# A two-layer decoder trunk on one core: transposes of queries, keys and attention weights move from TensorE to VectorE and the DMA queues

## The chip, the core and the metric

The kernel runs on one core of a Trainium2 chip, in one launch. The metric is the device time of the launch in microseconds, lower is better. All arithmetic is float32 at the interface; the large products are made of float32r parts.

## What is computed

One sequence of 256 tokens, width 2048. Layer 0 is a gated token mixer with a feed-forward part (width 5632, causal convolution of width 3); layer 1 is an attention with forget gates and a feed-forward part of the same kind. The change concerns the attention of layer 1, cut here to what it computes:

```python
kvf = rmsnorm(h, kv_norm) @ w_kvf            # keys, values and 16 forget gates, one side for all
k, v, f = ...                                # 16 heads of 128
k = rmsnorm(k, k_norm)                       # per head
c = cumsum(log_sigmoid(f + b_f))             # one row of 256 sums per head
q, g = split(rmsnorm(h, b_norm) @ w_qg)
q = rmsnorm(q, q_norm)                       # per head
for i in range(2):                           # query blocks of 128 tokens
    s = q[i] @ k[:hi].T * 128**-0.5 + c[t] - c[s]
    p = softmax(where(s_index <= t_index, s, -inf))
    o[i] = p @ v[:hi]
h = h + (o * sigmoid(g)) @ w_out
```

## The kernel before

**The stream.** All weights pass through one list of chunks, each 128 x 1024 floats (512 KB), in the order in which they are used. `Stream.run` goes through the list once. In its turn i it issues the load of chunk i+6 (line 70, on SyncE's queue, into one of four buffers `raw`), splits chunk i+3 (lines 82 and 83: ScalarE writes the high part `whi`, VectorE the low part `wlo` = raw - whi, four buffers each), emits the products of chunk i on TensorE (line 166), and then takes every pending generator one step further (`advance`). A generator's step is all it emits up to its next `yield`. So the place of every other instruction, on each engine and on the queues, is set by the turn in which its generator reaches it, and each engine works through its own list in that order. The load of chunk i+6 needs the buffer of chunk i+2, so it waits until VectorE has split that one.

**The products.** Each is high x high, low x high and high x low. In a token block (512 output columns for all 256 tokens, 8 chunks, 12 matmuls of 512 columns per chunk) the second matmul of a chunk already reads the low part.

**The attention.** The stages, in order: four token blocks of queries (`b_q`), one small chunk of forget gates (`kvf_f`), four blocks of keys (`kvf_k`), four of values (`kvf_v`), then the output gates (`b_g`, 8 groups of 4 chunks) and the output projection (`b_out`). Beside the first query chunks `kv_operand` prepares the second operand `att_X` from the residual `h`, one of 16 rows of blocks per turn (`prep`, lines 258 and 259). `forget_sums` makes the gates' sums on VectorE in many small steps (lines 609 to 644), during the first 20 turns of the keys.

**Norm of queries and keys.** When a block of queries or keys is done, `head_norm` squares its first 128 tokens on ScalarE (line 561), reduces and takes the reciprocal root on VectorE (lines 564 to 567, small operations), and scales out of PSUM (line 569). Two turns later TensorE transposes the four heads by matmuls with the identity `ident` (line 575) into a small PSUM bank `mp`, and ScalarE copies them, times the norm's gain, to `att_q` or `att_k` (line 576). In the turn after that the same begins for the second 128 tokens.

**Heads.** `heads` starts one generator `one_head` every second turn, as soon as the head's values are there. A head: fetch its row of sums broadcast to all partitions (line 650, GpSimd's queue), the bias of sums and mask in `L` (lines 655 to 658), scores on TensorE (660, 661), softmax (663 to 671), three transposes of the weights on TensorE (676) and their copy to `att_pT` on ScalarE (678), output on TensorE (683 to 685), its copy over the head's queries in `att_q` (686). Each head takes three of the two rotating `mp` banks in turn. The output gates (`g_done`) wait until all 16 heads are done, then follow one per turn.

## Time and profile before

| what | value |
|---|---|
| median of 3 runs | 2210.79 us (2210.58 to 2210.93) |
| the profiled execution, its own time | 2210.51 us |
| its span in the trace | 2208.8 us |
| granted TensorE clock | 0.999 |
| busy: PE, DVE, ACT, POOL | 2199.4, 1465.0, 1154.1, 19.0 us |
| query and key blocks, 1003 to 1192 us | PE 189.0, DVE 143.4, ACT 93.2 us busy |
| values and heads, 1192 to 1342 us | PE 150.0, DVE 91.9, ACT 91.2 us busy |

How to read it: PE is TensorE's matmuls, PEld its weight loads, DVE VectorE, ACT ScalarE, POOL GpSimd, SP SyncE; a q behind a name (SPq) is that engine's instruction queue, where DMAs are issued. In a row of a group stand the line of the kernel, the engine, the operation, output and inputs, shapes and the count; behind the bar the busy time in us and the mean of one in ns; behind the second bar the idle time just before, with what ended it. In a timeline a row begins with start and length in us. Matmuls overlap in the pipeline, so a step from one start to the next says more than a length. In a row of a stage (`A:B`) stand its length and then busy time and count for PE, PEld, DVE, ACT and POOL, the clock, the DMA engines' busy share and GB/s. DMA rows end with the median time from issue to landing.

### The profile page before, as it was taken

The page shows a single profiled execution, that of the slowest core. Times are in us where ns is not written, and L with a number is a line of the kernel's source. Part 1 is how long each engine was busy: PE and PEld are TensorE (multiplying, and loading weights), DVE is VectorE, ACT ScalarE, POOL GpSimd, SP SyncE. Part 2 cuts the span into 40 slices and gives each one's busy share as a digit, 9 for nine tenths or more (in the row PEclk, how much of TensorE's full clock was granted, in tenths as well). Part 3 has the DMA queues.
Part 4 walks back from the last instruction along what each step waited for, and adds up shares of the span by engine and source line. Part 5 has one row for each costly group of instructions (what it writes and reads, how often), then busy time and mean ns, then how long its engine had stood idle before and what let it go on. Part 6 is the DMA issues. An engine that isn't in the chain of part 4 may idle for free.

```text
span 2208.8 us, 41643 instructions
## 1 busy us (share of the span) xinstructions
PE 2199.4 (100%) x17208; PEld 2105.5 (95%) x17208; DVE 1465.0 (66%) x2107; ACT 1154.1 (52%) x1549; POOL 19.0 (1%) x41
## 2 busy tenths in 40 slices
PE   9999999999999999999999999999999999999998
PEld 7899999999999999998788888999999999999998
DVE  6676677777777755557786566667777777765553
ACT  5545455555555544345444666556555555544443
POOL 0000000000000000000000110000000000000000
PEclk9999999999999999999999999999999999999999
DMA  8555565556555655665565555656556565655653
GB/s 304 178 192 178 195 196 196 192 194 197 192 191 195 197 191 184 207 192 172 174 186 185 173 163 184 195 189 195 191 194 196 187 198 194 198 192 194 195 192 134
DMA packets 116910, 422.70 MB, mean 191 GB/s; under 512 B 13280, under 2 KB 13680, under 8 KB 116464
## 3 DMA queue, kind: packets, MB, share of 16 engines
q1 hardware_dynamic: 115776, 417.93, 57.8%
q8 instruction: 134, 2.20, 0.4%
q0 software_dynamic: 768, 2.10, 0.4%
q14 instruction: 56, 0.46, 0.1%
q10 hardware_dynamic: 176, 0.02, 0.0%
HBM read 417.88 MB, written 2.11 MB: 190 GB/s over the span
## 4 chain that ended last, share of the span: by engine, by line
PE 99%; DMA 0%; DVE 0%; ACT 0%; ACTq 0%; issue 0%; SPq 0%; DVEq 0%
PE ps L166 96%; PE mp L166 1%; DMA raw<-a_in_v 0%; PE mp L489 0%; PE mp L575 0%; PE mp L661 0%; PE mp L676 0%; PE mp L685 0%; PE mp L684 0%; PE mp L660 0%; PE mp L683 0%; PE mp L350 0%; DVE h L402 0%; DVE wlo L83 0%; ACT whi L82 0%; ACTq L811 0%
## 5 line engine op out<-in xcount | busy, mean ns | idle before, releaser
L83 DVE TENSOR_TENSOR wlo<-raw,whi 128x1024 fp32r<-128x1024 f32 (+1 forms) x787 | 954.8, 1219 | 461.1 <-ACT whi L82 459.3
L82 ACT ACTIVATE whi<-raw 128x1024 fp32r<-128x1024 f32 (+1 forms) x787 | 826.8, 1056 | 670.9 <-PE ps L166 602.4
L166 PE MATMUL ps<-X,whi 128*128 128x256 f32 (+1 forms) x6176 | 827.8, 286 | 0.0
L166 PEld LDWEIGHTS ps<-X,whi 128*128 128x128 f32 x6176 | 758.3, 188 | 16.5
L166 PE MATMUL ps<-X,wlo 128*128 128x256 f32 x3328 | 445.5, 276 | 0.0
L166 PEld LDWEIGHTS ps<-X,wlo 128*128 128x128 f32 x3328 | 413.2, 188 | 5.5
L166 PE MATMUL ps<-ffn_H,whi 128*128 128x256 f32 (+1 forms) x2696 | 342.9, 277 | 0.0
L166 PEld LDWEIGHTS ps<-ffn_H,whi 128*128 128x128 f32 x2696 | 322.7, 188 | 1.1
L166 PE MATMUL ps<-ffn_H,wlo 128*128 128x256 f32 x1364 | 186.6, 276 | 0.0
L166 PEld LDWEIGHTS ps<-ffn_H,wlo 128*128 128x128 f32 x1364 | 170.2, 188 | 0.4
L166 PE MATMUL ps<-whi,att_X 128*128 128x512 f32 x512 | 168.1, 400 | 0.0
L523 DVE SCALAR_TENSOR_TENSOR ffn_c<-ffn_a,col,ffn_c 128x255 f32<-128x255 f32 x352 | 162.0, 481 | 6.3
L166 PE MATMUL ps<-whi,X 128*128 128x512 f32 x512 | 161.6, 395 | 0.5 <-ACT whi L82 0.5
L519 ACT ACTIVATE ffn_c<-ffn_a,col 128x256 f32<-128x256 f32 x176 | 96.4, 595 | 49.8 <-DVE ffn_a L316 49.8
L166 PEld LDWEIGHTS ps<-whi,X 128*128 128x128 f32 x512 | 96.0, 188 | 21.9 <-ACT whi L82 1.2
L166 PEld LDWEIGHTS ps<-whi,att_X 128*128 128x128 f32 x512 | 96.2, 188 | 20.4
L316 DVE TENSOR_TENSOR ffn_a<-ps,rB 128x512 f32<-128x512 f32 x74 | 51.2, 692 | 96.7 <-PE ps L166 96.7
L166 PE MATMUL ps<-wlo,X 128*128 128x512 f32 x256 | 99.4, 391 | 0.8 <-DVE wlo L83 0.8
L166 PE MATMUL ps<-wlo,att_X 128*128 128x512 f32 x256 | 100.0, 390 | 0.0
L258 ACT ACTIVATE X<-h,col 128x256 fp32r<-128x256 f32 x64 | 29.1, 501 | 84.4 <-DVE h L322 67.8
L166 PE MATMUL ps<-att_X,whi 128*128 128x256 f32 (+2 forms) x520 | 68.9, 281 | 0.0
L166 PEld LDWEIGHTS ps<-att_X,whi 128*128 128x128 f32 (+1 forms) x520 | 61.5, 185 | 2.2
(160 smaller groups left out, 1156.3 us busy)
## 6 DMA issues: line engine op xcount, KB each, us to landing
raw<-up SPq DMA_DIRECT2D x352, 512.0 KB, 3.4
raw<-down SPq DMA_DIRECT2D x176, 512.0 KB, 4.1
raw<-a_in_u SPq DMA_DIRECT2D x32, 512.0 KB, 3.9
raw<-a_out SPq DMA_DIRECT2D x32, 512.0 KB, 4.2
raw<-b_q SPq DMA_DIRECT2D x32, 512.0 KB, 4.2
raw<-kvf_k SPq DMA_DIRECT2D x32, 512.0 KB, 4.2
raw<-kvf_v SPq DMA_DIRECT2D x32, 512.0 KB, 4.0
raw<-b_g SPq DMA_DIRECT2D x32, 512.0 KB, 3.3
```

Of the source, the lines that this page charges most:

```text
L82: self.nc.scalar.activation(hi[:, :n], raw, AF.Copy)
L83: self.nc.vector.tensor_tensor(lo[:, :n], raw, hi[:, :n].bitcast(F32), op=OP.subtract)
L166: nc.tensor.matmul(o, a, b, start=start, stop=stop, skip_group_check=True)
L258: nc.scalar.activation(dst[:, kt, :T], h[:, kt, :], AF.Copy, scale=g)
L316: nc.vector.tensor_tensor(a, src, rB[:, None, :].to_broadcast([P, 2, T]), op=OP.mult)
L519: nc.scalar.activation(c[:, m, :], a[:, m, :], AF.Identity, scale=w[2], bias=column(C_CONVB + l * 2 * KF + f))
L523: nc.vector.scalar_tensor_tensor(c[:, m, n:], a[:, m, :T - n], w[k], c[:, m, n:], op0=OP.mult, op1=OP.add)
```

## The change

Three things are done. First, the transposes leave TensorE. `blocks_turned` transposes on VectorE in blocks of 32 x 32, which turns each block but leaves the blocks where they are; `exchange` moves the blocks between groups of 32 partitions by way of a DRAM buffer `way`: four writes of 32 partitions each, in the next turn, and one read in the turn after, all on SyncE's queue. Keys land directly in `att_k` (in an order of 32-token blocks, which the score matmuls read with strides); queries land in a buffer `att_rows` of 128 x 512, and ScalarE copies them to `att_q` three turns after the read, times the product of both norms' gains (`att_gain`, made once); weights land in `att_rows` and are read by the output matmuls directly.

Second, `head_norm` has one `yield` where there were three: the transpose of the first 128 tokens and the norm of the second 128 follow in the turn after the first norm.

Third, `one_head` and `heads` become one generator. It takes two turns per head, starts when the keys are done (before, a head waited for its values), fetches the row of sums for the next head ahead, and emits in the first turn of head n the output of an earlier head (at most n-3) ahead of the scores of n, two outputs per round once all scores are out. The output gates of heads 2p and 2p+1 wait for those two heads only. GpSimd's descriptor scratch is set to 4096 bytes.

```diff
-    def head_norm(key, blk, gain):
+    def blocks_turned(src, n):
+        turned = ph.temp("turned", [P, 512])[:, :n * P].rearrange("p (c h j) -> p c h j", c=4, h=n)
+        nc.vector.transpose(turned.rearrange("p c h j -> p h c j"),
+                            src.rearrange("p (h c i) -> p h c i", h=n, c=4))
+        return turned.rearrange("p c h j -> p c (h j)")
+
+    def exchange(key, turned, n, new, then):
+        way = dram.tile([4, 32, 4, n * 32], F32, name=f"way_{key}", tag=f"way_{key}")
+        for r in range(4):
+            nc.sync.dma_start(way[:, :, r, :].rearrange("c i x -> i c x"), turned[32 * r:32 * r + 32])
+        yield
+        dst = new()
+        nc.sync.dma_start(dst, way.rearrange("c i r x -> (c i) r x"))
+        yield
+        then(dst)
+
+    def head_norm(key, blk):
...
                 yield
-                yield
-                mp = misc_ps()
-                for j in range(4):
-                    nc.tensor.transpose(mp[:, j * P:(j + 1) * P], n[:, j * P:(j + 1) * P], ident)
-                nc.scalar.activation(dst[:, 4 * blk:4 * blk + 4, tb * P:(tb + 1) * P],
-                                     mp.rearrange("p (a b) -> p a b", a=4), AF.Copy, scale=column(gain))
-                yield
+                turned = blocks_turned(n, 4)
+                if key == "k":
+                    new = lambda tb=tb: att("k").rearrange("p b t h j -> p b t (h j)")[:, blk, 4 * tb:4 * tb + 4]
+                    s.start(exchange(f"k{blk}{tb}", turned, 4, new, lambda dst: None))
+                else:
+                    s.start(exchange(f"q{blk}{tb}", turned, 4, lambda: four_rows(4),
+                                     lambda dst, tb=tb: s.start(q_scaled(blk, tb, dst))))
...
+    def four_rows(n):
+        return ph.temp("rows", [P, 512], bufs=6)[:, :n * P].rearrange("p (r x) -> p r x", r=4)
+
+    def q_scaled(blk, tb, rows):
+        yield
+        nc.scalar.activation(att("q")[:, 4 * blk:4 * blk + 4, tb * P:(tb + 1) * P].rearrange(
+            "p h (r j) -> p r h j", r=4), rows.rearrange("p r (h j) -> p r h j", h=4), AF.Copy, scale=att("gain"))
...
-    def one_head(hd):
...
-        mp = misc_ps()
-        for j in range(3):
-            nc.tensor.transpose(mp[:, j * P:(j + 1) * P], L[:, j, :], ident)
-        pT = ph.temp("pT", [P, 3, P])
-        nc.scalar.activation(pT, mp[:, :3 * P].rearrange("p (a b) -> p a b", a=3), AF.Copy)
...
+        while state["done"] < NH:
...
+            go = [hd for hd, _ in waiting if hd < min(state["v"], n - 2)][:2 if n >= NH else 1]
+            o = misc_ps() if go else None
+            for i, hd in enumerate(go):
+                pT = waiting.pop(0)[1]
+                oo, vv = o[:, i * T:(i + 1) * T], v[:, :, hd * P:(hd + 1) * P]
+                nc.tensor.matmul(oo[:, :P], vv[:, 0, :], pT[:, :, 0, :], start=True, stop=True)
+                nc.tensor.matmul(oo[:, P:], vv[:, 0, :], pT[:, :, 1, :], start=True, stop=False)
+                nc.tensor.matmul(oo[:, P:], vv[:, 1, :], pT[:, :, 2, :], start=False, stop=True)
+            if n < NH:
+                S = misc_ps()[:, :3 * P]
+                kk = k[:, n // 4, :, n % 4, :]
+                nc.tensor.matmul(S[:, :P], q[:, n, :P], kk[:, :4], start=True, stop=True)
+                nc.tensor.matmul(S[:, P:], q[:, n, P:], kk, start=True, stop=True)
+            for i, hd in enumerate(go):
+                nc.scalar.activation(q[:, hd, :], o[:, i * T:(i + 1) * T], AF.Copy)
+                state["done"] += 1
+            yield
...
+                s.start(exchange(f"p{n}", blocks_turned(L, 3), 3, lambda: four_rows(3),
+                                 lambda dst, n=n: waiting.append((n, dst.rearrange("p r (b j) -> p r b j", b=3)))))
...
-            while state["done"] < NH or state["gates"] < p:
+            while state["done"] < 2 * p + 2 or state["gates"] < p:
...
-    nc = bacc.Bacc("TRN2", target_bir_lowering=False, num_devices=1)
+    nc = bacc.Bacc("TRN2", target_bir_lowering=False, num_devices=1, dynamic_dma_scratch_size=4096)
```

VectorE's list at the end of the first query block, before: from the end of the first norm (line 569) to the begin of the second (line 564). `att_big` is the scaled result, `wlo` a chunk's low part, `att_X` the operand being prepared.

```order
L569 TENSOR_TENSOR att_big<-ps,att_hr 128x512
L83 TENSOR_TENSOR wlo<-raw,whi 128x1024
L259 SCALAR_TENSOR_TENSOR att_X_11579<-h,col,att_X_11579 128x256
L83 TENSOR_TENSOR wlo<-raw,whi 128x1024
L259 SCALAR_TENSOR_TENSOR att_X_11579<-h,col,att_X_11579 128x256
L83 TENSOR_TENSOR wlo<-raw,whi 128x1024
L259 SCALAR_TENSOR_TENSOR att_X_11579<-h,col,att_X_11579 128x256
L564 TENSOR_REDUCE att_hv<-sq 128x4
```

The same place after the change, from the operand's prep (line 259) to the end of the second norm and on to its transpose; the lines of the norm are now 584 to 589, the transpose is 551.

```order
L259 SCALAR_TENSOR_TENSOR att_X_11505<-h,col,att_X_11505 128x256
L551 STREAM_TRANSPOSE att_turned<-att_big 128x4x4x32
L584 TENSOR_REDUCE att_hv<-sq 128x4
...
L587 TENSOR_SCALAR att_hr<-att_hr,rcol 128x4
L589 TENSOR_TENSOR att_big<-ps,att_hr 128x512
L83 TENSOR_TENSOR wlo<-raw,whi 128x1024
L259 SCALAR_TENSOR_TENSOR att_X_11505<-h,col,att_X_11505 128x256
L551 STREAM_TRANSPOSE att_turned<-att_big 128x4x4x32
```

Between the two norms stood three low parts; now one stands there (ahead of the first row shown), and the transpose.

SyncE's list after the change, in the stage of the values: `raw` is a weight load, `way_p` a head's four writes, the row that reads `way_p` its read. Before, this stage held nothing but the 32 loads.

```order
L70 DMA raw<-kvf_v 128x1024
L559 DMA way_p_13423<-att_turned 32x4x96 x4
L70 DMA raw<-kvf_v 128x1024
L562 DMA att_rows<-way_p_13423 128x384
L70 DMA raw<-kvf_v 128x1024
L559 DMA way_p_13489<-att_turned 32x4x96 x4
```

Each head puts five DMAs between two loads and the next two: the writes behind one load, the read behind the other.

TensorE's list in a head, before: the transposes (line 676) cut through a chunk, and the output (683 to 685) and the scores of the next head (660, 661) follow behind it.

```order
L166 MATMUL ps<-whi,att_X_11579 128x512
L676 MATMUL mp<-ident,att_big 128x128 x3
L166 MATMUL ps<-whi,att_X_11579 128x512
...
L683 MATMUL mp<-att_pT,att_v 128x128
L684 MATMUL mp<-att_pT,att_v 128x128
L685 MATMUL mp<-att_pT,att_v 128x128
L660 MATMUL mp<-att_k,att_q 128x128
L661 MATMUL mp<-att_k,att_q 128x256
```

The same place after the change.

```order
L166 MATMUL ps<-whi,att_X_11505 128x512
L705 MATMUL mp<-att_rows,att_v 128x128
L706 MATMUL mp<-att_rows,att_v 128x128
L707 MATMUL mp<-att_rows,att_v 128x128
L711 MATMUL mp<-att_k,att_q 128x128
L712 MATMUL mp<-att_k,att_q 128x256
L166 MATMUL ps<-whi,att_X_11505 128x512
```

The transposes are gone from the list; output and scores stand as before, with the weights read from `att_rows`.

More of the change, by code (lines that the diff above doesn't have):

```diff
@@ L542, in att @@
         ph.open("att")
-        shape = {"X2": [P, KD, 2 * T], "q": [P, NH, T], "k": [P, NH, T], "v": [P, 2, D],
-                 "ccol": [P, 2, NH]}[key]
+        shape = {"X2": [P, KD, 2 * T], "q": [P, NH, T], "k": [P, 4, 8, 4, 32], "v": [P, 2, D],
+                 "ccol": [P, 2, NH], "gain": [P, 1]}[key]
         return ph.keep(key, shape, F32R if key == "X2" else F32)
+    def blocks_turned(src, n):
[12 more added lines that the diff above has]
+        then(dst)
     def kv_operand():
+        att("X2")
+        nc.vector.tensor_tensor(att("gain"), column(C_QNORM), column(C_KNORM), op=OP.mult)
         for _ in range(3):
@@ L552, in kv_operand @@
             yield
-    def head_norm(key, blk, gain):
+    def head_norm(key, blk):
         def done(ps):
-            dst = att(key)
             for tb in range(2):
@@ L587, in done @@
             yield
-            for hd in range(4 * blk, 4 * blk + 4):
-                state["heads"].append(hd)
+            state["v"] += 4
         return done
@@ L645, in forget_sums, with heads @@
         yield
-    def one_head(hd):
+    def heads():
         q, k, v, ccol = att("q"), att("k"), att("v"), att("ccol")
-        cB = ph.temp("cB", [P, T])
-        nc.gpsimd.dma_start(cB, cd[hd:hd + 1, :].to_broadcast([P, T]))
-        yield
-        L = ph.temp("big", [P, 512], bufs=6)[:, :3 * P].rearrange("p (a b) -> p a b", a=3)
-        mp = misc_ps()
-        S = mp[:, :3 * P]
-        nc.scalar.activation(L[:, 0, :], cB[:, :P], AF.Identity, scale=-1.0, bias=ccol[:, 0, hd:hd + 1])
-        nc.scalar.activation(L[:, 1:, :], cB.rearrange("p (a b) -> p a b", a=2), AF.Identity, scale=-1.0,
-                             bias=ccol[:, 1, hd:hd + 1])
-        nc.gpsimd.affine_select(L[:, 0::2, :], L[:, 0::2, :], pattern=[[0, 2], [-1, P]], compare_op=OP.is_ge,
-                                fill=NEG, base=0, channel_multiplier=1)
-        nc.tensor.matmul(S[:, :P], q[:, hd, :P], k[:, hd, :P], start=True, stop=True)
-        nc.tensor.matmul(S[:, P:], q[:, hd, P:], k[:, hd, :], start=True, stop=True)
-        yield
-        nc.vector.scalar_tensor_tensor(L, S.rearrange("p (a b) -> p a b", a=3), SCALE, L, op0=OP.mult, op1=OP.add)
-        mx = ph.temp("mx", [P, 2])
-        sm = ph.temp("sm", [P, 2])
-        for tb, part in ((0, L[:, 0:1, :]), (1, L[:, 1:3, :])):
-            nc.vector.tensor_reduce(mx[:, tb:tb + 1], part, axis=AX.XY, op=OP.max, negate=True)
-            nc.scalar.activation(part, part, AF.Exp, bias=mx[:, tb:tb + 1], accum_out=sm[:, tb:tb + 1])
-        nc.vector.reciprocal(sm, sm)
-        for tb, part in ((0, L[:, 0:1, :]), (1, L[:, 1:3, :])):
-            nc.vector.tensor_scalar(part, part, sm[:, tb:tb + 1], None, op0=OP.mult)
-        yield
-        yield
-        mp = misc_ps()
-        for j in range(3):
-            nc.tensor.transpose(mp[:, j * P:(j + 1) * P], L[:, j, :], ident)
-        pT = ph.temp("pT", [P, 3, P])
-        nc.scalar.activation(pT, mp[:, :3 * P].rearrange("p (a b) -> p a b", a=3), AF.Copy)
-        yield
-        mp = misc_ps()
-        o = mp[:, :T]
-        vv = v[:, :, hd * P:(hd + 1) * P]
-        nc.tensor.matmul(o[:, :P], vv[:, 0, :], pT[:, 0, :], start=True, stop=True)
-        nc.tensor.matmul(o[:, P:], vv[:, 0, :], pT[:, 1, :], start=True, stop=False)
-        nc.tensor.matmul(o[:, P:], vv[:, 1, :], pT[:, 2, :], start=False, stop=True)
-        nc.scalar.activation(q[:, hd, :], o, AF.Copy)
-        state["done"] += 1
@@ L689, in heads, with fetch @@
-    def heads():
-        n = 0
-        while n < NH:
-            if state["heads"]:
-                s.start(one_head(state["heads"].pop(0)))
-                n += 1
-                yield
-            yield
+        parts = [(0, 0, 1), (1, 1, 3)]
+        rows, waiting = {}, []
+        def fetch(hd):
+            rows[hd] = ph.temp("cB", [P, T])
+            nc.gpsimd.dma_start(rows[hd], cd[hd:hd + 1, :].to_broadcast([P, T]))
+        fetch(0)
+        yield
+        n = 0
+        while state["done"] < NH:
+            if n < NH:
+                cB = rows.pop(n)
+                L = ph.temp("big", [P, 512], bufs=6)[:, :3 * P]
+                l = L.rearrange("p (a b) -> p a b", a=3)
+                nc.scalar.activation(l[:, 0, :], cB[:, :P], AF.Identity, scale=-1.0, bias=ccol[:, 0, n:n + 1])
+                nc.scalar.activation(l[:, 1:, :], cB.rearrange("p (a b) -> p a b", a=2), AF.Identity, scale=-1.0,
+                                     bias=ccol[:, 1, n:n + 1])
+                nc.gpsimd.affine_select(l[:, 0::2, :], l[:, 0::2, :], pattern=[[0, 2], [-1, P]],
+                                        compare_op=OP.is_ge, fill=NEG, base=0, channel_multiplier=1)
+                if n + 1 < NH:
+                    fetch(n + 1)
+            go = [hd for hd, _ in waiting if hd < min(state["v"], n - 2)][:2 if n >= NH else 1]
[6 more added lines that the diff above has]
+                nc.tensor.matmul(oo[:, P:], vv[:, 1, :], pT[:, :, 2, :], start=False, stop=True)
+            if n < NH:
+                S = misc_ps()[:, :3 * P]
[5 more added lines that the diff above has]
+                state["done"] += 1
+            yield
+            if n < NH:
+                nc.vector.scalar_tensor_tensor(L, S, SCALE, L, op0=OP.mult, op1=OP.add)
+                mx = ph.temp("mx", [P, 2])
+                sm = ph.temp("sm", [P, 2])
+                for tb, a, b in parts:
+                    nc.vector.tensor_reduce(mx[:, tb:tb + 1], l[:, a:b, :], axis=AX.XY, op=OP.max, negate=True)
+                    nc.scalar.activation(l[:, a:b, :], l[:, a:b, :], AF.Exp, bias=mx[:, tb:tb + 1],
+                                         accum_out=sm[:, tb:tb + 1])
+                nc.vector.reciprocal(sm, sm)
+                for tb, a, b in parts:
+                    nc.vector.tensor_scalar(l[:, a:b, :], l[:, a:b, :], sm[:, tb:tb + 1], None, op0=OP.mult)
+                s.start(exchange(f"p{n}", blocks_turned(L, 3), 3, lambda: four_rows(3),
+                                 lambda dst, n=n: waiting.append((n, dst.rearrange("p r (b j) -> p r b j", b=3)))))
+            yield
+            n += 1
@@ L715, in build @@
     tail = {}
-    state = {"normed": False, "layer": 0, "heads": [], "done": 0, "gates": 0}
+    state = {"normed": False, "layer": 0, "v": 0, "done": 0, "gates": 0}
     cd = dram.tile([NH, T], F32, name="cd")
@@ L742, in build @@
     for blk in range(4):
-        tok_block(d["b_q"][8 * blk:8 * blk + 8], lambda: X1, head_norm("q", blk, C_QNORM))
+        tok_block(d["b_q"][8 * blk:8 * blk + 8], lambda: X1, head_norm("q", blk))
     s.chunk(d["kvf_f"], forget)
     for blk in range(4):
-        tok_block(d["kvf_k"][8 * blk:8 * blk + 8], lambda: att("X2"), head_norm("k", blk, C_KNORM))
+        tok_block(d["kvf_k"][8 * blk:8 * blk + 8], lambda: att("X2"), head_norm("k", blk))
     s.then(at_mult=lambda: s.start(heads()))
```

## The prediction

> **What bounds the kernel now.** I read the page first: busy time by engine, then the chain that ended last.

> ```profile
> span 2208.8 us, 41643 instructions
> PE 2199.4 (100%) x17208; PEld 2105.5 (95%) x17208; DVE 1465.0 (66%) x2107; ACT 1154.1 (52%) x1549; POOL 19.0 (1%) x41
> ...
> PE 99%; DMA 0%; DVE 0%; ACT 0%; ACTq 0%; issue 0%; SPq 0%; DVEq 0%
> ```

> TensorE is the chain from end to end, so whatever leaves it shortens the kernel, and whatever another engine does costs nothing until TensorE waits for it. So I priced the transposes on the chain (in order of time; start, length), once in a query block and once in a head:

> ```profile
> 1025.85 8.26 PE ps L166 x36
> 1034.11 0.44 PE mp L575 x4
> ...
> 1234.11 2.77 PE ps L166 x12
> 1236.88 0.33 PE mp L676 x3
> 1237.20 2.77 PE ps L166 x12
> ...
> 1241.30 2.77 PE ps L166 x12
> ```

> The groups by line give the counts:

> ```profile
> L575 PE MATMUL mp<-ident,att_big 128*128 128x128 f32 x64 | 9.6, 273 | 0.0
> ...
> L676 PE MATMUL mp<-ident,att_big 128*128 128x128 f32 x48 | 7.8, 272 | 0.0
> ```

> 64 in fours and 48 in threes are 16 pieces of each kind: 16 x 0.44 + 16 x 0.33 = 7.04 + 5.28 = 12.3 us on the path. All of them go; the order of TensorE holds neither any more. That is the whole gain there is, and TensorE's other work stays the same in number and size. The profiled execution took 2210.51 us (1.7 around its span; 0.28 under the median 2210.79), and I sum against it: 2198.2 if nothing new is waited for.

> **What VectorE's new order costs.** Before, the two norms of a token block lay three chunks apart; now the second follows one chunk after the first, with a transpose between. TensorE holds three split chunks in hand. Whether they last is a walk through VectorE's queue, on the timeline of the first query block (t = 0 where the square starts):

> ```profile
> 1019.94 0.69 ACT L561 ACTIVATE sq<-ps,rcol 128x512 f32<-128x512 f32 x1 [1.29 <-PE ps L166]
> 1019.98 0.39 PE L166 MATMUL ps<-wlo,X 128*128 128x512 f32 x1
> ...
> 1020.66 0.69 DVE L564 TENSOR_REDUCE att_hv<-sq 128x4 f32<-128x512 f32 x1 [0.75 <-ACT sq L561]
> ...
> 1022.72 0.39 PE L166 MATMUL ps<-wlo,X 128*128 128x512 f32 x1
> ...
> 1023.90 0.69 DVE L569 TENSOR_TENSOR att_big<-ps,att_hr 128x512 f32<-128x512 f32 x1
> ...
> 1024.51 1.22 DVE L83 TENSOR_TENSOR wlo<-raw,whi 128x1024 fp32r<-128x1024 f32 x1
> ...
> 1025.64 0.48 DVE L259 SCALAR_TENSOR_TENSOR att_X<-h,col,att_X 128x256 fp32r<-128x256 f32 x1
> ...
> 1026.04 1.22 DVE L83 TENSOR_TENSOR wlo<-raw,whi 128x1024 fp32r<-128x1024 f32 x1
> ...
> 1029.10 0.68 DVE L564 TENSOR_REDUCE att_hv<-sq 128x4 f32<-128x512 f32 x1
> ...
> 1032.87 1.22 DVE L83 TENSOR_TENSOR wlo<-raw,whi 128x1024 fp32r<-128x1024 f32 x1
> ```

> Call the block's last chunk i. TensorE's first use of the low part falls 0.04 after t = 0 in chunk i+1 and a chunk is 2.74 long, so the low part of chunk i+5 is needed at 0.04 + 4 x 2.745 = 11.02. VectorE in the new order: first norm ends 4.57 (1024.51); low part of i+4 1.13; operand prep 0.40, to 6.10; transpose; second norm 3.77 (1029.10 to 1032.87); low part of i+5, 1.22. The transpose isn't in this trace. An operation over 128x512 occupies VectorE for 0.61 (1023.90 to 1024.51). The bounds:

> ```profile
> L83 DVE TENSOR_TENSOR wlo<-raw,whi 128x1024 fp32r<-128x1024 f32 x782 | 951.7, 1223 | 458.8 <-ACT whi L82 457.0
> ...
> L671 DVE TENSOR_SCALAR att_big<-att_big,att_sm 128x256 f32<-128x256 f32 x16 | 5.6, 347 | 0.0
> ```

> From 0.35 (half the columns) to 1.14 (twice; 1.22 with its tail). I take 0.61, the same size. Then 6.10 + 0.61 + 3.77 + 1.22 = 11.70: 0.68 late. That holds for query blocks 0 and 1, where the prep runs. Blocks 2 of the queries and 1 to 3 of the keys have no prep: 11.30, 0.28 late each. Query block 3 is followed by the gates' chunk, and is covered:

> ```profile
> 1088.63 0.69 ACT L561 ACTIVATE sq<-ps,rcol 128x512 f32<-128x512 f32 x1 [1.69 <-PE ps L166]
> ...
> 1094.19 0.37 ACT L609 ACTIVATE att_big<-ps 16x256 f32<-16x256 f32 x1 [3.92 <-PE ps L166]
> ```

> 5.5 us instead of 2.7 pass there. In key block 0 the gates' series stands in the same queue:

> ```profile
> 1121.67 1.22 DVE L83 TENSOR_TENSOR wlo<-raw,whi 128x1024 fp32r<-128x1024 f32 x1
> 1122.81 0.41 DVE L628 TENSOR_TENSOR att_big<-att_big 16x256 f32<-16x256 f32 x1
> ...
> 1123.46 1.21 DVE L83 TENSOR_TENSOR wlo<-raw,whi 128x1024 fp32r<-128x1024 f32 x1
> ```

> 1.79 from low part to low part instead of 1.13: 0.94 late. Sum 2 x 0.68 + 4 x 0.28 + 0.94 = 3.4 us, seven new waits of TensorE for VectorE (at the transpose's bounds 1.6 to 7.1).

> [...]

> **What SyncE's queue costs.** Every exchange puts four writes and a read on the queue that issues the weight loads, in order. The writes hold the queue until VectorE has transposed, the read until the writes have landed, and the loads stand behind both.

> ```profile
> 2.18 0.43 SPq L412 DMA_DIRECT2D h<-xT  x1
> ...
> 1072.67 0.33 SPq L70 DMA_DIRECT2D raw<-kvf_f  x1
> ...
> raw<-b_q SPq DMA_DIRECT2D x32, 512.0 KB, 4.2
> out<-h SPq DMA_DIRECT2D x2, 256.0 KB, 2.2
> cd<-att_big ACTq DMA_DIRECT2D x1, 16.0 KB, 3.6
> ...
> L82 ACT ACTIVATE whi<-raw 128x1024 fp32r<-128x1024 f32 x782 | 823.8, 1059 | 669.4 <-PE ps L166 602.4 <-issue 16.1 <-ACT whi L82 12.6
> ```

> In a block without prep: second transpose done about 11.9; a load and a read go out with it (0.4 each); four writes at 0.4 end about 13.7; they land 2.2 (output, 256 KB, nothing beside it) to 3.6 us later (16 KB among loads); read at 15.9 to 17.3; the next load at 16.3 to 17.7, landed 4.2 later, 20.5 to 21.9; high part 1.06; so its low part occupies VectorE until 22.7 to 24.1. The next block's first norm could start at 8 x 2.745 + 0.3 + 0.72 = 23.0. It starts 0 to 1.1 late, and that is added whole to that block's wait. It concerns query blocks 1 and 2 and key blocks 1 to 3: 0 to 5.5 us. The rows stand on both sides, so I take 0.5 each, 2.5 in all.

> During the heads I cost the queue at nothing. The stage's row, and the queue's:

> ```profile
> 1205.00:1340.00 135.00, 135.00 (x731) 115.78 (x731) 81.16 (x142) 83.21 (x177) 15.13 (x31) 1.00 0.54 169
> ...
> q1 hardware_dynamic: 115776, 417.93, 57.8%
> att_cB<-cd POOLq DMA_DIRECT2D x16, 128.0 KB, 3.6
> ```

> A head takes 7.19 (1234.11 to 1241.30) and will take 6.86. VectorE (81 of 135) and ScalarE (83) have room for a transpose. Queue 1 moves 418 MB in 57.8% of 2208.8 us, 327 GB/s, so 192 KB each way is 1.2 us, and 46% of 7.19, 3.3 us, is free. The output matmuls use an exchange three heads, some 17 us, after its transpose, against about 8 for its writes and read. The row of sums is fetched one head ahead: 3.6 against 6.9. Weights now leave SyncE at most a few us later, which the three split chunks hide.

> At nothing too: the key and weight evictions that leave ScalarE, the query's that becomes a copy from SBUF of the same size, one 128x1 multiply, the strided reads of keys and weights by TensorE (as many columns), the smaller descriptor scratch (GpSimd is 1% busy), and gates that no longer wait for all heads: TensorE did not wait there before.

> Sum: 2210.5 - 12.3 + 3.4 + 2.5 = 2204.1 us.

> **Rivals.**
> - **All of it is kept**: the transpose is short and loads land early, TensorE waits nowhere: 2198.2. For it: no wait of TensorE stands in the chain now. Against: the walk has no reserve in seven places. 17%.
> - **The cover is gone altogether**: the transpose at 1.14 adds 7 x 0.53 = 3.7, the loads' lateness at its upper end 5.5: 2198.2 + 3.4 + 3.7 + 5.5 = 2210.8. The gain is eaten; VectorE's burst bounds the token blocks. Against: 128x512 rows agree on 0.61. [...] 20%.
> - **SyncE's round trip bounds the heads (slower)**: per head its queue needs 1.6 for writes, L until they land, 0.4 and 0.35 for read and load: 2.35 + L against 6.86, so it falls behind from L = 4.5. A load leaves some seven chunks of 3.4 before its use, less 4.2 landing and 2.3 split, so about 16 us can be lost before TensorE notices. At L = 6.5 it loses 2.0 x 16 = 32, 16 of them on TensorE: 2220. It outweighs the gain from about L = 5.9. Against: 2.2, 3.6, 4.2 are the rows. For it: four small writes behind each other among loads. 12%. [...]

> That the transposes stay on TensorE is excluded by its order.

> **How the numbers follow.** The forecast has 51%, its own range 2199.8 (waits of 1.6 and no late load) to 2207.1 (3.4 and 5.5). 0.2% is 4.4 us, about what a measurement of this kernel can tell, so faster means under 2206.4. Faster: 0.44 of the forecast's 0.51, the first rival's 0.17, 0.01 of the second: 0.62. Same: 0.07, 0.17 and 0.01 of the slow one: 0.25. Slower: 0.13, most of the third and the second's far end. The range 2198 to 2214 leaves out the third rival and little else.

> **What would show it.** Right: no matmul with ident in the query blocks and heads; in the waits, TensorE idle for the low part (wlo, VectorE) about seven times, 0.3 to 2 us each, near the ends of token blocks; transposes of about 0.69; in the heads no TensorE idle time. Wrong: transposes over 1.2 us; writes landing later than 4.5; TensorE idle in the values' and gates' stages; or no idle time at all, and a span near 2196.

## The result: slower by 0.5%, and the profile after

The changed kernel takes 2221.48 us (median of 5 runs, 2217.78 to 2222.46) against 2210.79 before: ratio 1.0046, 95% interval 1.0031 to 1.006. That is 17 us above the forecast of 2204.1 and outside its range, 2198 to 2214. The profiled execution took 2217.78 us. Its page, with busy time and the chain by engine:

```profile
span 2216.1 us, 41701 instructions
PE 2193.7 (99%) x17096; PEld 2097.0 (95%) x17096; DVE 1481.1 (67%) x2140; ACT 1142.3 (52%) x1525; POOL 24.0 (1%) x41
...
PE 90%; DVE 4%; DMA 3%; issue 1%; ACT 1%; SPq 0%; ACTq 0%; DVEq 0%; POOL 0%; POOLq 0%
```

The 112 transposes are gone (17208 matmuls before, 17096 now), but the chain, 99% TensorE before, now leaves it for a tenth of the span. What TensorE waited for, in order (us in total, times, longest):

```profile
PE ps L166 <- DVE wlo L83: 12.0, 8, 2.9
PE mp L711 <- DVE att_big L718: 2.2, 1, 2.2
...
SPq L562 <- DMA way_k<-att_turned: 8.1, 10, 1.7
SPq L562 <- DMA way_q<-att_turned: 6.3, 6, 1.9
```

The first row is the low part of the weights, which VectorE makes (counted at the weight loads, PEld, it is 16.6 us, the figure that the expectations use); the second a head's scores at the start of the heads. The last two are SyncE's own: its reads stand until their writes have landed. TensorE's rows with a wait in brackets, one behind the end of each token block (queries 0, 1, 2; keys 0, 1, 2, 3):

```profile
1031.38 0.50 PE L166 MATMUL ps<-wlo,X 128*128 128x512 f32 x1 [0.55 <-DVE wlo L83]
1056.70 0.50 PE L166 MATMUL ps<-wlo,X 128*128 128x512 f32 x1 [2.85 <-DVE wlo L83]
1081.12 0.50 PE L166 MATMUL ps<-wlo,X 128*128 128x512 f32 x1 [2.18 <-DVE wlo L83]
...
1132.97 0.50 PE L166 MATMUL ps<-wlo,att_X 128*128 128x512 f32 x1 [2.02 <-DVE wlo L83]
1160.10 0.50 PE L166 MATMUL ps<-wlo,att_X 128*128 128x512 f32 x1 [2.46 <-DVE wlo L83]
1184.63 0.51 PE L166 MATMUL ps<-wlo,att_X 128*128 128x512 f32 x1 [0.67 <-DVE wlo L83]
1203.15 0.50 PE L166 MATMUL ps<-wlo,att_X 128*128 128x512 f32 x1 [1.08 <-DVE wlo L83]
```

The waits stand where the forecast put them; the first one is as small as the walk said, the second five times as long as the first. Slices of 2 us behind two of these waits (span; busy PE, PEld, DVE, ACT, POOL; then granted clock, DMA share, GB/s):

```profile
1134.00:1136.00 2.00, 2.00 (x6) 1.63 (x5) 1.97 (x5) 0.00 (x0) 0.00 (x0) 0.50 0.92 298
1136.00:1138.00 2.00, 2.00 (x7) 1.54 (x7) 1.97 (x4) 0.80 (x1) 0.00 (x0) 0.64 0.94 272
...
1162.00:1164.00 2.00, 2.00 (x7) 1.52 (x6) 2.00 (x2) 0.00 (x0) 0.00 (x0) 0.50 0.92 322
1164.00:1166.00 2.00, 2.00 (x9) 1.62 (x8) 0.84 (x2) 1.06 (x1) 0.00 (x0) 0.82 0.91 262
...
1252.00:1380.00 128.00, 128.00 (x703) 110.48 (x702) 86.00 (x130) 75.59 (x134) 10.99 (x17) 1.00 0.71 220
```

Behind the 2.02 and the 2.46 the clock was halved for some 3.4 us (behind the 2.46 it was at 0.83 in 1160 to 1162 already): 1.0 + 0.7 = 1.7 us lost each time. Behind the 2.85 and the 2.18 it stayed at 1.00. The last row is the heads once they run: no idle time at all.

The balance against the profile before: 2217.78 - 2210.51 = +7.3, and 12.3 of transposes are gone, so 19.6 us came in. TensorE's idle time grew from 9.4 (2208.8 - 2199.4) to 22.4: 13.0. Its busy time is 6.6 above 2199.4 - 12.3; 3.4 of that are the two spells of halved clock. Half of the other 3.2 stands in e5_start too, a run below in which nothing waits any more (busy 2188.7, 1.6 above the same 2187.1), so 1.6 us go with the waits and have no row of their own.

### The profile page after: what moved, and what is told of

It is laid out like the page before. It is cut to its first block, busy times and chain, and to the rows that moved or that the text cites. A ratio compares the mean times of both kernels' runs of the same rounds, so it can differ in the third digit from the quotient of the medians.

```text
span 2216.1 us, 41701 instructions
## 1 busy us (share of the span) xinstructions
PE 2193.7 (99%) x17096; PEld 2097.0 (95%) x17096; DVE 1481.1 (67%) x2140; ACT 1142.3 (52%) x1525; POOL 24.0 (1%) x41
## 3 DMA queue, kind: packets, MB, share of 16 engines
q8 instruction: 133, 2.18, 0.4%
## 4 chain that ended last, share of the span: by engine, by line
PE 90%; DVE 4%; DMA 3%; issue 1%; ACT 1%; SPq 0%; ACTq 0%; DVEq 0%; POOL 0%; POOLq 0%
PE ps L166 88%; DVE wlo L83 1%; DMA raw<-kvf_k 1%; PE mp L166 1%; DMA raw<-b_q 1%; ACT whi L82 1%; DMA way_k<-att_turned 0%; DVE att_turned L551 0%; DVE att_hv L584 0%; PE mp L489 0%; DMA raw<-kvf_v 0%; DVE rs_t L275 0%; DVE rs_t L274 0%; DVE att_hr L276 0%; DMA way_q<-att_turned 0%
## 5 line engine op out<-in xcount | busy, mean ns | idle before, releaser
L83 DVE TENSOR_TENSOR wlo<-raw,whi 128x1024 fp32r<-128x1024 f32 (+1 forms) x787 | 954.1, 1218 | 455.4 <-ACT whi L82 453.6
L82 ACT ACTIVATE whi<-raw 128x1024 fp32r<-128x1024 f32 (+1 forms) x787 | 826.2, 1056 | 693.4 <-PE ps L166 590.0
L166 PE MATMUL ps<-X,whi 128*128 128x256 f32 (+1 forms) x6176 | 826.3, 285 | 0.0
L166 PEld LDWEIGHTS ps<-X,whi 128*128 128x128 f32 x6176 | 757.9, 188 | 16.2
L166 PE MATMUL ps<-X,wlo 128*128 128x256 f32 x3328 | 445.3, 276 | 0.0
L166 PEld LDWEIGHTS ps<-X,wlo 128*128 128x128 f32 x3328 | 413.0, 188 | 5.5
L166 PE MATMUL ps<-ffn_H,whi 128*128 128x256 f32 (+1 forms) x2696 | 342.9, 277 | 0.0
L166 PEld LDWEIGHTS ps<-ffn_H,whi 128*128 128x128 f32 x2696 | 322.6, 188 | 1.1
L166 PE MATMUL ps<-ffn_H,wlo 128*128 128x256 f32 x1364 | 186.7, 276 | 0.0
L166 PEld LDWEIGHTS ps<-ffn_H,wlo 128*128 128x128 f32 x1364 | 170.2, 188 | 0.4
L166 PE MATMUL ps<-whi,att_X 128*128 128x512 f32 x512 | 167.3, 403 | 0.0
L166 PE MATMUL ps<-whi,X 128*128 128x512 f32 x512 | 160.9, 395 | 0.0
L166 PEld LDWEIGHTS ps<-whi,att_X 128*128 128x128 f32 x512 | 97.6, 191 | 21.1
L166 PEld LDWEIGHTS ps<-whi,X 128*128 128x128 f32 x512 | 96.6, 189 | 20.9 <-ACT whi L82 0.3
L166 PE MATMUL ps<-wlo,att_X 128*128 128x512 f32 x256 | 101.9, 398 | 6.6 <-DVE wlo L83 6.4
L166 PE MATMUL ps<-wlo,X 128*128 128x512 f32 x256 | 99.6, 392 | 5.6 <-DVE wlo L83 5.6
L166 PE MATMUL ps<-att_X,whi 128*128 128x256 f32 (+2 forms) x520 | 68.9, 281 | 0.0
L166 PEld LDWEIGHTS ps<-wlo,att_X 128*128 128x128 f32 x256 | 49.0, 191 | 19.6 <-DVE wlo L83 9.0
## 6 DMA issues: line engine op xcount, KB each, us to landing
raw<-up SPq DMA_DIRECT2D x352, 512.0 KB, 3.3
raw<-down SPq DMA_DIRECT2D x176, 512.0 KB, 4.3
raw<-a_in_u SPq DMA_DIRECT2D x32, 512.0 KB, 3.6
raw<-a_out SPq DMA_DIRECT2D x32, 512.0 KB, 4.1
raw<-b_q SPq DMA_DIRECT2D x32, 512.0 KB, 4.1
raw<-kvf_k SPq DMA_DIRECT2D x32, 512.0 KB, 4.7
raw<-kvf_v SPq DMA_DIRECT2D x32, 512.0 KB, 4.8
raw<-b_g SPq DMA_DIRECT2D x32, 512.0 KB, 4.2
```

The lines of the kernel that those rows point to most:

```text
L82: self.nc.scalar.activation(hi[:, :n], raw, AF.Copy)
L83: self.nc.vector.tensor_tensor(lo[:, :n], raw, hi[:, :n].bitcast(F32), op=OP.subtract)
L166: nc.tensor.matmul(o, a, b, start=start, stop=stop, skip_group_check=True)
```

## The experiments

Expectations speak of three theories: A, the loads stand behind exchanges in SyncE's in-order queue; B, VectorE's burst of two norms; C, the exchanges' traffic itself.

**Four kernels on one chip: take the queue's wait away, take the burst away, both, and leave the exchange out.**

```
exchange, for queries and keys:            # e1_late, e3_both
+        for _ in range(2): yield          # ahead of the writes
...
+        for _ in range(2): yield          # ahead of the read
head_norm, at the loop's end:              # e2_spread, e3_both
+                yield
+                yield
head_norm, in place of both exchanges:     # e4_nodma
                 if key == "k":
+                    nc.scalar.activation(att("k").rearrange("p b t h j -> p b t (h j)")[:, blk, 4 * tb:4 * tb + 4],
+                                         turned, AF.Copy)
                 else:
+                    s.start(q_scaled(blk, tb, turned))
```

> In the query and key blocks the writes of an exchange leave two turns later and its read two more turns later, so that SyncE no longer stands before them; VectorE's burst of two norms is unchanged, and so are the heads. Theory A (SyncE's queue, where the loads stand behind an exchange whose read waits for its writes, is the larger term): the read's waits for way_q and way_k (14.4 us together in the changed kernel) go, raw lands as before, and of TensorE's 16.6 us of waits for wlo about the 3.4 us of my walk are left: 2217.8 - 13 = about 2205. Theory B (VectorE's burst is the larger term): the waits for wlo stay at 14 to 17 us, 2216 to 2222. Theory C (the 128 KB each way slow the loads wherever they stand in the queue): waits of 10 to 17 us stay and raw keeps landing late, 2213 to 2222.

> The second norm of a token block starts three turns after the first, as in the kernel before, with the transposes on VectorE and the exchanges as in the changed kernel (no wait is taken from SyncE). Theory B (the burst): TensorE's waits for wlo fall from 16.6 to under 3 us, 2201 to 2205. Theory A (SyncE's queue): the loads are late as before, since each read still waits for its writes; only the walk's 3.4 us go, and waits of 9 to 13 us stay, 2210 to 2217. Theory C as A.

> Both edits together: later writes and reads, and the norms three turns apart. A and B together: no wait of TensorE for wlo beyond 1 us in sum; what stays is the wait of 2.4 us at the heads' start: 2198.2 + 2.4 = about 2201, and faster than before. C: waits stay where the traffic is, 2205 or more.

> The query and key blocks leave the exchange out (writes, read and what the quadrants trade; the keys and queries so stand in the wrong places); VectorE still transposes, and ScalarE copies the transposed tile to the keys or queries. The heads are as in the changed kernel. It prices VectorE's burst by itself. Theory A: the walk's 3.4 us of waits for wlo are left (1.6 to 7.1), 2198.2 + 3.4 + 2.4 at the heads' start = about 2204. Theory B: 13 to 17 us are left, about 2216.

Measured: e1_late 2213.12 (ratio 1.0009, 1.0 to 1.0018), e2_spread 2202.82 (0.9962, 0.9947 to 0.9977), e3_both 2205.68 (0.9976, 0.9966 to 0.9985), e4_nodma 2218.93 (1.0034, 1.0021 to 1.0046).

No theory alone fits: e2_spread's time is the one that B forecast, e1_late's lies between A's and B's. In the query blocks A does. TensorE's rows of e1_late, then slices of e4_nodma over the first three query blocks:

```profile
1031.51 0.50 PE L166 MATMUL ps<-wlo,X 128*128 128x512 f32 x1 [0.54 <-DVE wlo L83]
1054.34 0.50 PE L166 MATMUL ps<-wlo,X 128*128 128x512 f32 x1 [0.58 <-DVE wlo L83]
1076.75 0.50 PE L166 MATMUL ps<-wlo,X 128*128 128x512 f32 x1 [0.15 <-DVE wlo L83]
...
1153.09 0.50 PE L166 MATMUL ps<-wlo,att_X 128*128 128x512 f32 x1 [2.12 <-DVE wlo L83]
```

```profile
1012.00:1036.00 24.00, 23.46 (x103) 18.95 (x102) 19.56 (x47) 14.60 (x21) 0.00 (x0) 1.00 0.45 145
1036.00:1060.00 24.00, 23.44 (x103) 18.93 (x102) 21.45 (x47) 13.18 (x19) 0.00 (x0) 1.00 0.58 188
1060.00:1084.00 24.00, 23.86 (x104) 19.27 (x103) 16.89 (x39) 11.16 (x13) 0.00 (x0) 1.00 0.56 190
```

With all the bytes but no block in the queue: 0.54, 0.58, 0.15. With no bytes at all: 0.54, 0.56, 0.14. So the traffic costs nothing there (C falls), the burst costs 1.3 us, and the other 4.3 of the 5.6 us in the changed kernel's query blocks are the queue. e1_late also lets ScalarE's copy of the queries come later. In the changed kernel that copy waits for its read too, but the load lands later still, so it is the load that counts there (ScalarE at the end of query block 0):

```profile
1041.68 0.72 ACT L607 ACTIVATE att_q<-att_rows,att_gain 128x512 f32<-128x512 f32 x1 [1.40 <-DMA att_rows<-way_q]
1043.06 1.06 ACT L82 ACTIVATE whi<-raw 128x1024 fp32r<-128x1024 f32 x1 [0.66 <-DMA raw<-b_q]
```

In the key blocks e4_nodma can't be read: its copy of the keys stands in ScalarE's queue and waits for VectorE's transpose (39.6 us in 8 waits, the longest 5.4), ahead of the high parts, a wait that the changed kernel hasn't.

But e2_spread, which leaves SyncE's waits alone, has no wait for wlo in any block. Its SyncE waits even longer for the keys' writes than the changed kernel's 8.1 us, and TensorE doesn't notice:

```profile
SPq L562 <- DMA way_k<-att_turned: 16.4, 11, 4.3
...
PE mp L713 <- DVE att_big L720: 2.7, 2, 2.2
```

The queue's lateness counts only because the burst has used up the split chunks in hand. e3_both is slower than e2_spread by 2.9. All its waits are at the heads' start: 4.1 us (1.9 for the values' eviction, 2.2 for scores), with the clock at 0.73 in the 8 us around them and 0.85 in the next 8. The last key block's exchanges now fall there, and VectorE's transpose of a head's weights has to wait for one of them, since the two buffers `turned` are shared:

```profile
1212.79 0.58 DVE L551 STREAM_TRANSPOSE att_turned<-att_big 128x384 f32<-128x384 f32 x1 [2.33 <-DMA way_k<-att_turned]
```

The changed kernel and e2_spread have no such wait of VectorE there. So this part of e3_both's time comes from its own delay of the writes.

**The heads' start, the two halves of the change, and another queue.**

```
heads:                                     # e5_start = e2_spread and this
+        for _ in range(4): yield          # ahead of fetch(0)
head_norm: as before, keys copied into the new layout   # e6_heads
heads: as before (one_head); norms as e2_spread         # e7_qk
exchange, for queries and keys:            # e8_pool
-            nc.sync.dma_start(...)
+            nc.gpsimd.dma_start(...)      # writes and read
```

> As e2_spread, and the heads begin four turns later. In e2_spread TensorE still waits 2.2 us once, for the fifth head's scores, because VectorE comes to the third and fourth heads' softmax late, behind the last key block's norms. If that lag is the cause, the wait goes and the time is 2202.8 - 2.4 = about 2200.4 (1.4 to 2.6 less than e2_spread). If the lag is the heads' own (the rows of sums that land late, the values' evictions), the wait of 2 us comes four turns later all the same: 2202 to 2204.

> Only the heads are changed; queries and keys are transposed by TensorE with the norms three turns apart, as before (the keys' eviction writes the new layout). 5.3 us of transposes go. If the heads cost nothing else: 2205.2. With the wait at their start that e2_spread kept (2.4 us): about 2207.6. With a start as in e1_late (5.7 us of waits): 2210 to 2211.

> The complement with the norms three turns apart: queries and keys by VectorE and exchange, each head as before with TensorE's three transposes. 7.0 us go: 2203.5 if the token blocks wait for nothing, as in e2_spread. If exchanges that stand in SyncE's queue cost something that e2_spread's profile does not show as a wait, 2205 to 2208.

> The changed kernel with only the queue of the query and key exchanges changed: their writes and reads are issued by GpSimd, so that no load stands behind one; burst, turns and bytes are those of the changed kernel. Theory A (order in SyncE's queue): the query blocks' waits for wlo fall from 5.6 us to the burst's 1.3 that e1_late and e4_nodma left, and the time to that of e1_late, 2210 to 2213. Theory C (the traffic itself): they stay above 4 us, 2215 to 2222.

Measured: e5_start 2198.84 (2198.57 to 2199.59; ratio 0.9947, 0.9934 to 0.9959), e6_heads 2206.26 (0.9979, 0.9971 to 0.9988), e7_qk 2204.62 (0.9973, 0.9963 to 0.9984), e8_pool 2220.08 (1.0043, 1.0029 to 1.0057). The lag was the cause of the wait at the heads' start: VectorE begins them behind the last key block's norms. Its removal brought 4.0, more than the wait. The two halves pay 4.5 and 6.2 by themselves, near their 5.3 and 7.0 (e6_heads still waits 1.5 us at the heads' start). TensorE in e5_start, the query, key and value blocks and the heads, in two slices:

```profile
1000.00:1256.00 256.00, 255.85 (x1153) 208.58 (x1152) 205.30 (x451) 133.82 (x198) 13.25 (x20) 1.00 0.71 225
1256.00:1400.00 144.00, 143.80 (x872) 126.86 (x871) 98.06 (x138) 82.84 (x133) 8.07 (x13) 1.00 0.67 211
```

0.35 us idle in 400, clock 1.00. This version beats both kernels, the one before by 12.0 us: nearly all of the 12.3.

e8_pool missed: 7.0 us of waits stayed in the query blocks, and by its time alone it would speak for C. Its rows of ScalarE show why, the second being a single copy that holds ScalarE for 5.36:

```profile
ACT att_q L607 <- DMA att_rows<-way_q: 14.4, 4, 5.4
...
1044.72 0.72 ACT L607 ACTIVATE att_q<-att_rows,att_gain 128x512 f32<-128x512 f32 x1 [5.36 <-DMA att_rows<-way_q]
```

No load stood behind the exchange any more; ScalarE's high parts did instead, behind the queries' copy, three turns after a read that hadn't landed. The keys have no such copy, and there the waits fell to 2.6 us.

**The same with the copy later, the burst by itself, and the clock.**

```
q_scaled:                                  # e9_pool_copy = e8_pool and this
-        yield
+        for _ in range(4): yield
e10_late_start: e1_late, with the four turns of e5_start
up_done, at its end, in the kernel before: # e11_stall
+            if i % 4 == 2: stall(2 * (i // 4) + 4)
+    def stall(n):
+        for _ in range(n): nc.vector.tensor_scalar(t, t, 1.0, None, op0=OP.mult)
+        nc.tensor.transpose(mp[:, :P], t[:, :P], ident)
```

> As e8_pool, and ScalarE's copy of the queries waits three turns longer, so that it no longer stands before its read has landed (14.4 us of waits of ScalarE in e8_pool, in the query blocks alone). Theory A, widened (a load or a high part that stands in any in-order queue behind the exchange's round trip is late): the query blocks' waits for wlo fall from 7.0 us to the burst's 1.3, the key blocks stay at e8_pool's 2.6, and the time is 2220.1 - 5.8 - 1.7 to 3.4 of granted clock, 2211 to 2213. Theory C (traffic): 5 us or more stay in the query blocks, 2217 to 2220.

> e1_late with the heads begun four turns later: the burst alone, without the queue's and the heads' start's waits. The walk gave 3.4 us for it; e1_late showed 4.6 (the first key block after the gates' 1.1, the second 2.1, where the gates' series still runs). 2198.2 + 4.6 = 2202.8, and 2204.5 if one of the waits lowers the granted clock. If the heads' start costs as much as in e1_late: 2208 or more.

> The kernel before, in whose first up stage VectorE does 4, 6, 8 ... 24 idle 128x256 multiplies after every fourth block (11 places) and TensorE then transposes their tile, so that it waits for a growing time with nothing else changed. It asks for the granted clock alone. If a wait of TensorE itself lowers the clock, it falls for some 3.5 us (about 1.7 us lost) behind the waits of 2 us and more, and not behind shorter ones. If the lowered clock in the changed kernel came from other load (transfers, VectorE), it stays at 1.00 here.

e9_pool_copy: 2209.76 (0.9996, 0.9986 to 1.0005), as A widened said and a little under its range. The bytes and their queue are e8_pool's, so the traffic by itself wasn't what held e8_pool up. TensorE's waits in the query blocks:

```profile
1031.65 0.50 PE L166 MATMUL ps<-wlo,X 128*128 128x512 f32 x1 [0.56 <-DVE wlo L83]
1054.49 0.50 PE L166 MATMUL ps<-wlo,X 128*128 128x512 f32 x1 [0.59 <-DVE wlo L83]
1076.95 0.50 PE L166 MATMUL ps<-wlo,X 128*128 128x512 f32 x1 [0.19 <-DVE wlo L83]
```

e10_late_start: 2205.98 (0.9981, 0.9973 to 0.999), 3 us over my 2202.8, although its waits for wlo (5.8 us) were near the forecast and the clock stayed at 1.00 from 1020 to 1324; 1.3 us are new, output matmuls that wait for an exchange after the later start.

Four medians now part the loss, each step taking away one thing more: 2221.48 (changed) - 2213.12 (queue freed) = 8.4; 2213.12 - 2205.98 (heads later) = 7.1; 2205.98 - 2198.84 (norms apart) = 7.1. The kernel before took 2210.48 to 2210.85 beside them, so the four can be compared. But the parts aren't independent. With the norms apart the heads' start costs 4.0 and the queue nothing. And part of the 7.1 for the heads' start was brought in by e1_late itself, whose delayed writes meet the heads as in e3_both:

```profile
1206.27 0.58 DVE L551 STREAM_TRANSPOSE att_turned<-att_big 128x384 f32<-128x384 f32 x1 [2.92 <-DMA way_k<-att_turned]
```

TensorE waits 5.7 us there, with a spell of low clock behind (0.79 in 1220 to 1228), against 3.5 us (1.3 for the low part, 2.2 for scores) and no such spell in the changed kernel. So 7.1 is too much for the changed kernel's own heads' start, and 8.4 too little for the queue. e9_pool_copy frees SyncE's queue without delaying the writes: 2221.48 - 2209.76 = 11.7.

Waiting is not all that is lost: the clock behind a wait can fall too. e11_stall shows it: 2337.96 us. The edit ran in both up stages, so there were 22 places, not 11; TensorE waited 78.8 us in them. Three of its transposes with their waits, and then the clock behind the third:

```profile
366.30 0.33 PE L514 MATMUL mp<-ident,still 128*128 128x128 f32 x1 [0.83 <-DVE still L512]
411.85 0.33 PE L514 MATMUL mp<-ident,still 128*128 128x128 f32 x1 [1.63 <-DVE still L512]
458.00 0.33 PE L514 MATMUL mp<-ident,still 128*128 128x128 f32 x1 [2.28 <-DVE still L512]
...
458.00:460.00 2.00, 2.00 (x12) 2.00 (x13) 1.07 (x1) 0.00 (x0) 0.00 (x0) 0.69 0.03 8
460.00:462.00 2.00, 2.00 (x11) 2.00 (x11) 0.00 (x0) 0.69 (x1) 0.00 (x0) 0.50 0.72 262
...
core 0: 2339.2 us, clock 0.978
```

The kernel grew by 127.5 us. In its profile (130.5 us longer than the one before) TensorE's idle time grew by 79.1 and its busy time by 51.3 (2250.7 - 2199.4). At 0.33 (the rows above) to 0.44 each (the one behind a wait of 2.94) the 22 added transposes are some 7 to 10 of these; the rest, 40 us or more, goes with the mean clock of 0.978 instead of 0.999. So waiting by itself can lower the clock.

## Why the prediction was wrong, step by step

- **The gain, 12.3 us: right.** e5_start, with no wait left, took 2198.84; the sum without waits was 2198.2 on a profile that lies 0.28 under its median.
- **The transpose's size: right.** Taken 0.61, bounds 0.35 to 1.14. In the chain each holds the path for 0.62 (its full length is the 0.70 below):

```profile
L551 DVE STREAM_TRANSPOSE att_turned<-att_big 128x512 f32<-128x512 f32 x16 | 11.2, 703 | 0.0
L551 DVE STREAM_TRANSPOSE att_turned<-att_big 128x384 f32<-128x384 f32 x16 | 9.3, 579 | 0.5
```
- **The burst, 3.4 us: right in sum, one block mis-sized.** With the queues free (e9_pool_copy) TensorE waited 3.5 us for the low part, in six places:

```profile
PE ps L166 <- DVE wlo L83: 3.5, 6, 1.1
```

  In e1_late the query blocks waited 0.54, 0.58, 0.15 for my 0.68, 0.68, 0.28, and key block 0 1.08 for my 0.94. Key block 1 is the one that I had wrong: 1.08 in e9_pool_copy and 2.12 in e1_late for 0.28. I had the gates' series in block 0 alone, and it runs on into block 1. ScalarE of e1_late there (its queue, then the late square):

```profile
1141.37 0.34 ACTq L670 DMA_DIRECT2D cd<-att_big  x1
1141.75 0.69 ACT L586 ACTIVATE sq<-ps,rcol 128x512 f32<-128x512 f32 x1 [2.26 <-DVE att_big L669]
```

  The send of the sums waits on ScalarE for VectorE's scan, and the first square stands behind it. Before, the three turns between the norms absorbed that. As the last of the three steps above the burst is worth 7.1 us of time; 1.3 of it are e10_late_start's waits for an exchange.
- **SyncE's queue, 2.5 us (0 to 5.5): the step that failed; 7.5 us of waits, 8.4 to 11.7 us of time.** The waits for the low part are 12.0 us in the changed kernel and 4.5 in e1_late's token blocks. Key block 0, which I had not counted here, takes part (2.02 against 1.08). The order of events was as predicted, until the load. SyncE's queue in the changed kernel at the end of query block 0, then the chain of work behind it:

```profile
1032.37 1.88 SPq L559 DMA_DIRECT2D way_q<-att_turned  x4
...
1036.41 0.34 SPq L562 DMA_DIRECT2D att_rows<-way_q  x1
...
1036.84 6.12 DMA raw<-b_q
1043.06 1.07 ACT whi L82
1044.15 1.22 DVE wlo L83
1045.38 0.40 DVE att_X L259
1045.78 0.61 DVE att_hv L584
```

  From t = 0 at 1019.65 the writes end at 14.6 (13.7 taken, for a block without prep), the read goes at 16.8 (15.9 to 17.3), the load at 17.2 (16.3 to 17.7). But it landed 6.12 later, not 4.2: it was issued right behind a 256 KB read on the same queue. The 4.2 was the median of loads with nothing odd ahead of them. Then 0.4 of operand prep, which I had left out here, and the next norm begins at 1045.7. In e1_late it begins at 1043.34:

```profile
1043.34 0.68 DVE L589 TENSOR_REDUCE att_hv<-sq 128x4 f32<-128x512 f32 x1
```

  That is 2.4 late, twice the upper end of 1.1, and about the difference of the second query block's waits (2.85 - 0.58 = 2.3). The same load of e1_late stands behind four writes instead of the read; it was issued 0.8 earlier, at 1036.01, and took 1.5 less to land:

```profile
raw<-b_q SPq DMA_DIRECT2D x1, 512.0 KB, 4.6
```

  So the landing is the larger part of the lateness. That the read ahead of it is what slowed it is read from this order; no run changes the read alone.
- **The heads' start, costed at nothing: 2.2 us of waits in the changed kernel's trace, 4.0 us of time with the norms apart, 7.1 from e1_late with its own delay.** I looked at the heads as they run, which was right (128.00 of 128.00 us busy), and not at how they begin: the last key block's burst leaves VectorE behind, and the two small PSUM banks tie the scores to it (2.2 us for `att_big`).
- **The clock: not in the sum.** Two spells of 1.7 us in the profile.
- **Rivals.** "The cover is gone altogether" named the mechanism, but its price stopped at 2210.8, with the two upper ends added and nothing else. "SyncE's round trip bounds the heads" gave nearly the time that was measured, 2220, for a reason that the trace refutes: writes of a head landed 4.3 after issue (48 KB, under its threshold of 4.5, though longer than the 3.0 of the 64 KB writes of queries and keys), and the heads ran without a wait.

What stays open: the 1.6 us of TensorE's longer busy time that the clock's rows do not cover; how the loss parts exactly between the queue and the heads' start in the changed kernel, as no run delays the heads alone; and why the profiled execution was 4 us faster than the median; the other runs' mean clock is 0.996 or 0.997 against its 0.998, and 0.001 is 2.2 us, so another spell or two of low clock would do, but they have no trace.

## What to carry to other kernels

When a bound engine is relieved by handing work to others, walk the queues at the ends of blocks and at the start of the next stage, not the stage's mean: here the work fitted everywhere (VectorE 67% busy) and cost 22.6 us at the blocks' ends and the heads' start; two idle turns between the norms and four ahead of the heads, four lines of code, turned +0.5% into -0.5%. A round trip through memory should not stand ahead of anything urgent in any in-order queue, be it the one that issues it or the one that uses its result, unless enough work is in hand to cover it: with the norms apart it stayed in SyncE's queue and no low part was waited for (e2_spread). Price a wait of TensorE of 2 us or more above its length: behind those of 2.02 and 2.46 us here the lowered clock cost 1.7 us more each, behind those of 2.85 and 2.18 nothing.
